# One layer stack on one core: S5's direct term inside its kernels, z in three matmuls, S5's steps a head later, the border's chunks behind the scale

## The chip, the core and the metric

The kernel runs on one core of a Trainium2 chip. The metric is the device time of one execution in microseconds; the time of a kernel is the median over its runs. The engines named below are PE (TensorE, the matmuls), DVE (VectorE), ACT (ScalarE), POOL (GpSimd) and SP (SyncE, which issues most of the loads). Each works through its own queue in order, and waits on semaphores for the others.

## The reference

A batch of one, 256 positions of 2048 features, goes through four layers with a different mixer each. After each mixer stands a residual sum and a layer norm:

```python
for i in range(DEPTH):
    out = (ssd_mixer, fox_mixer, mla_mixer, s5_mixer)[i](h, ...)
    h = layer_norm(ALPHA * h + out, ln_g[i], ln_b[i])
```

SSD is a state-space mixer with a causal convolution and a chunked scan, Fox is attention with a cumulative forget gate, MLA is attention with low-rank queries and keys. The change touches S5 most:

```python
u, z = jnp.split(h @ w_in, 2, axis=-1)
lam_bar = jnp.exp(lam * step)
bu = jnp.einsum('gpi,btgi->btgp', b_bar, u.reshape(bsz, T, GROUPS, GROUP))
states = scan of  s[t] = lam_bar * s[t-1] + bu[t]          # complex, 64 states in each of 128 groups
y = einsum('gip,btgp->btgi', c, states).real.reshape(bsz, T, WIDTH) + d_skip * u
y = gelu(y)
y = y * sigmoid(y @ w_glu + b_glu)
y = y * silu(z)
return y @ w_out
```

The term `d_skip * u` is called the direct term below.

## The kernel before

**Matmuls.** Every product is made in three parts: a weight is split into a high and a low half (`whi` on ACT, L119; `wlo` on DVE, L120), the activations are split as well (`h`, two tiles that lie side by side), and high times high, high times low and low times high are summed. `half` loads one half of a weight tile (512 KB) into one of seven `raw` buffers and splits it; there are four `whi` and four `wlo`. `proj_T` makes an output with features on the partitions: per block of 128 inputs a matmul of 512 columns (L147: the high weight against both halves of the activations) and one of 256 (L148), into a PSUM tile `pT` whose two halves DVE then adds (L157). `proj_tok` makes outputs with positions on the partitions, in three matmuls of 512 columns (L126 to L128), in four column blocks `cb`. `proj_Tk` uses three matmuls of 256 columns (L212 to L214, tiles `pk`).

**The order of the work.** The program is written out once, in one order. Each `tick` (one half tile of weights) runs what had been deferred to it: `C.defer(n, fn)` runs `fn` n ticks later, and `C.behind` issues it behind the last matmul. Each engine then gets its own queue from that, so what is issued earlier stands ahead on its engine.

**Borders.** `out_layer` ends each layer: the output projection, the residual sum `resid` (L309) with statistics (L310), the scale `nm` from a Newton iteration on DVE (`stats`, rows `nt`, `ny`), `norm` in two passes over chunks of blocks (first pass L339 with the mean, second pass L340 with the scale `ny`), and the transposition for the next layer (`ptr`, L353, on PE; high half on ACT; low half `h` on DVE, L357). In the next layer's first projection PE has its first matmuls of L126 and L127 among the ptr, but L128 needs the low halves. Position block t = 1 comes last.

**SSD.** Per group of heads, `scores` multiplies the decays with the products of c and b (`cbp`, L567), `turn_x` transposes x (`xp`).

**S5's kernels, made during Fox.** `s5_params` is a generator that POOL, DVE and PE work through while Fox's heads run: in each of 16 groups POOL makes powers (`pn`, L1130 to L1139), and `turn` has PE transpose them and multiply them out (`wp`, L1070; `kp`, L1077) into the kernels of the short-range convolution (`kt`, stored to DRAM as K_d). The steps are called by `next(steps)`: one behind each of the last v strips (stripes of Fox's value projection), then one per head.

**S5's own stage.** Four strips `ft` of u are projected and turned; the scan over the states runs on DVE (tiles `X`, `sc`, L1207 to L1213), in pieces, `advance` issuing `SCAN_US` of it per tick; meanwhile PE makes the 16 tiles of z. Per strip, outputs of two kinds are summed: `near` from the short kernels (matrices `shifts`, from K_d) and `far` from the states (matrices `mats`, from P_d; the addition into `ys` is L1416). Then `back1` transposes (`yp`, L1425), ACT copies to `yt`, `back2` transposes again (`yp`, L1435), DVE adds the direct term (L1441), ACT takes gelu (L1450) and the result is split (L291, L292). The z tile is summed by L157, goes through tanh on ACT and a product on DVE (L1337). After the 16 tiles come the 16 of the gate (glu), then the output projection.

Of the kernel before, what the change touches and what calls it, by code (L numbers as in the profile page):

```python
# [30 lines left out]
class Core:  # L31
# [127 lines left out]
    def proj_tok(self, srcs, aT, n=512, before=None, tail=None, spare=None):  # L159
# [10 lines left out]
        while h < N:  # L170
# [123 lines left out]
    def out_layer(self, li, parts, gb_tiles, spare, out=None):  # L294
# [12 lines left out]
        def resid(t, cb, ps):  # L307
            r = self.hres[:, t, cb * 512:(cb + 1) * 512]
            V.scalar_tensor_tensor(r, r, ALPHA, ps, op0=ALU.mult, op1=ALU.add)  # L309
            V.bn_stats(st[:, t, cb, :], r)  # L310

        def stats(t):
            mv = self.tp.tile([P, 2], F32, tag="mv", name="mv", bufs=2)
            V.bn_aggr(mv, st[:, t])
# [6 lines left out]
            V.scalar_tensor_tensor(nm[t], mv[:, 0:1], -1.0, rs[t], op0=ALU.mult, op1=ALU.mult)  # L321
# [72 lines left out]
        for k0, nk in ((0, 2), (2, 2), (4, 4), (8, 4), (12, 4)):  # L394
            norm(1, k0, nk, 3)
# [55 lines left out]
def ssd(C, hT, out):  # L451
# [3 lines left out]
    with C.tc.tile_pool(name="ssd", bufs=1) as sp, C.tc.tile_pool(name="ssd_c", bufs=1) as vp, C.tc.tile_pool(name="ssd_t", bufs=1) as tp:  # L455
# [87 lines left out]
        def group(g):  # L543
# [111 lines left out]
def fox(C, hT, out):  # L655
# [3 lines left out]
    with pool(name="fox", bufs=1) as fp, pool(name="fox_t", bufs=2) as tp, \  # L659
# [49 lines left out]
        def head(h):  # L709
# [237 lines left out]
def s5_params(C, sp, sq):  # L947
# [118 lines left out]
    def turn(n, st, pn, d):  # L1066
# [5 lines left out]
        nc.scalar.copy(wt, wp.rearrange("p q b c f -> p (q b c f)"))  # L1072
        kp = C.aux("kp")
        for qq in range(2):
            for e in range(2):
                for c in range(2):
                    nc.tensor.matmul(kp[32 * qq:32 * qq + 32, e * 64:(e + 1) * 64], d[:, 2 * qq + e, c],  # L1077
                                     pn[:, c, 2 * qq + e, 0:4].rearrange("p r i -> p (r i)"), start=c == 0, stop=c == 1)
# [75 lines left out]
def s5(C, hT, out):  # L1154
# [8 lines left out]
    with C.tc.tile_pool(name="s5", bufs=1) as sp, C.tc.tile_pool(name="s5_w", bufs=1) as wp, C.tc.tile_pool(name="s5_t", bufs=1) as tp:  # L1163
        dT = sp.tile([P, KB], F32, name="dT")
        bg = sp.tile([P, KB], F32, name="bg")
        nc.sync.dma_start(dT, A["s5_dT"])
# [415 lines left out]
```

## Time and profile before

| | us |
|---|---|
| median of 3 runs | 2019.85 (2015.91 to 2023.44) |
| the profiled execution's own time | 2021.63 |
| its span, first to last instruction | 2019.8 |
| PE busy | 1970.5 (98%) |
| DVE busy | 1470.2 (73%) |
| ACT busy | 956.4 (47%) |
| POOL busy | 410.1 (20%) |
| mean granted TensorE clock | 0.991 |

The stages stand one after the other: SSD to about 709 us, Fox to 1233, MLA to 1581, S5 to the end; within S5 the u strips run from about 1600 to 1696, the z tiles to about 1826. Matmuls overlap, so the busy time of one is longer than the distance to the next; from which of the two a cost is worked out is said each time. A window's row has the busy time and the number of instructions of each engine, then the granted clock (1.00 is full speed), the DMA share and the rate. A row of the waits has the total, the number of times and the longest.

### The profile page before, as it was taken

What the parts mean: (1) busy time and instruction counts of PE and PEld (TensorE: products, weight loads), DVE (VectorE), ACT (ScalarE), POOL (GpSimd) and SP (SyncE); (2) the same over time, 40 slices, a digit from 0 to 9 for tenths busy, and PEclk for the clock granted to TensorE, in tenths of its full rate; (3) what the DMA queues carried; (4) which work ended last, traced back from release to release, by engine and by line L of the source; (5) the groups of instructions that cost most, each with busy time, mean ns of one, the idle gap of its engine ahead of it and who ended that gap; (6) DMA issues with size and microseconds to landing.
All of it is one profiled execution on the core that took longest, in us unless ns stands there. A gap on an engine that the chain in (4) does not pass through costs nothing.

```text
span 2019.8 us, 32021 instructions
## 1 busy us (share of the span) xinstructions
PE 1970.5 (98%) x12169; PEld 1684.2 (83%) x12169; DVE 1470.2 (73%) x2572; ACT 956.4 (47%) x1427; POOL 410.1 (20%) x482
## 2 busy tenths in 40 slices
PE   8999999999999999999999999999999999999997
PEld 6788888888888878788888888988988799878885
DVE  6788788887654596577777567666666778997856
ACT  5455555655433434344444443544654355445442
POOL 0101111011100027999993000000000000110002
PEclk9999999999999999999999999999999999999999
DMA  8555555555665546566566564655357456586552
GB/s 286 185 178 182 183 181 190 178 185 181 206 218 188 185 151 230 179 204 200 199 198 212 173 204 127 207 186 176 126 172 245 175 182 196 169 249 215 193 192 91
DMA packets 116235, 382.42 MB, mean 189 GB/s; under 512 B 18208, under 2 KB 20976, under 8 KB 114288
## 3 DMA queue, kind: packets, MB, share of 16 engines
q1 hardware_dynamic: 103424, 348.11, 52.0%
q0 software_dynamic: 7808, 26.56, 4.2%
q10 hardware_dynamic: 4848, 5.70, 0.8%
q8 instruction: 96, 1.57, 0.3%
q14 instruction: 59, 0.48, 0.1%
HBM read 366.20 MB, written 14.11 MB: 188 GB/s over the span
## 4 chain that ended last, share of the span: by engine, by line
PE 82%; DVE 10%; DMA 3%; POOL 2%; issue 2%; ACT 1%; SPq 0%; DVEq 0%; POOLq 0%; ACTq 0%
PE pT L147 24%; PE pT L148 12%; PE pt L127 10%; PE pt L128 10%; PE pt L126 10%; DVE wlo L120 3%; PE pk L212 2%; PE pk L214 2%; PE pk L213 2%; PE yd L602 1%; DVE hres L339 1%; DVE hres L340 1%; PE o L444 1%; DMA raw<-in_ssd_z 1%; PE kp L1077 1%
## 5 line engine op out<-in xcount | busy, mean ns | idle before, releaser
L120 DVE TENSOR_TENSOR wlo<-raw,whi 128x1024 fp32r<-128x1024 f32 (+4 forms) x612 | 749.5, 1227 | 350.1 <-ACT whi L119 343.7
L119 ACT CAST whi<-raw 128x1024 fp32r<-128x1024 f32 (+4 forms) x612 | 631.3, 1036 | 731.9 <-PE pt L128 320.7
L147 PE MATMUL pT<-h,whi 128*128 128x512 f32 (+2 forms) x2080 | 746.5, 401 | 0.0
L148 PE MATMUL pT<-h,wlo 128*128 128x256 f32 (+2 forms) x2080 | 585.7, 282 | 1.5 <-DVE wlo L120 1.5
L147 PEld LDWEIGHTS pT<-h,whi 128*128 128x128 f32 (+2 forms) x2080 | 389.9, 187 | 94.4 <-issue 0.2
L148 PEld LDWEIGHTS pT<-h,wlo 128*128 128x128 f32 (+2 forms) x2080 | 392.2, 189 | 3.2 <-DVE wlo L120 2.3
L126 PE MATMUL pt<-whi,h 128*128 128x512 f32 (+2 forms) x716 | 281.1, 393 | 6.3 <-ACT whi L119 6.0
L127 PE MATMUL pt<-wlo,h 128*128 128x512 f32 (+2 forms) x716 | 280.0, 391 | 5.8 <-DVE wlo L120 5.6
L128 PE MATMUL pt<-whi,h 128*128 128x512 f32 (+2 forms) x716 | 277.6, 388 | 0.3 <-DVE h L357 0.3
L127 PEld LDWEIGHTS pt<-wlo,h 128*128 128x128 f32 x716 | 136.4, 190 | 35.5 <-DVE wlo L120 8.9
L126 PEld LDWEIGHTS pt<-whi,h 128*128 128x128 f32 x716 | 136.2, 190 | 34.5 <-ACT whi L119 6.4
L128 PEld LDWEIGHTS pt<-whi,h 128*128 128x128 f32 x716 | 136.3, 190 | 26.7 <-issue 1.7
L589 POOL TENSOR_TENSOR xs<-xs,dsk 128x512 f32<-128x512 f32 x16 | 20.8, 1316 | 373.5 <-ACT xs L585 373.5
L126 PE MATMUL pt<-whi,yh 128*128 128x512 f32 x240 | 95.5, 398 | 0.0
L127 PE MATMUL pt<-wlo,yh 128*128 128x512 f32 x240 | 95.4, 397 | 0.0
L128 PE MATMUL pt<-whi,yl 128*128 128x512 f32 x240 | 94.9, 395 | 0.0
L147 PE MATMUL pT<-y,whi 128*128 128x512 f32 x256 | 90.9, 400 | 0.0
L1179 POOL DMA_DIRECT2D mats<-W_d x8 | 4.3, 542 | 336.1 <-DVE h L292 265.7
L148 PE MATMUL pT<-y,wlo 128*128 128x256 f32 x256 | 72.0, 281 | 0.0
L496 DVE SCALAR_TENSOR_TENSOR conv<-u,cw,conv 128x255 f32<-128x255 f32 x144 | 68.8, 479 | 2.2
L89 POOL MEMSET mask<- 128x256 f32 x2 | 0.6, 314 | 302.1 <-PE pt L128 164.4
L147 PEld LDWEIGHTS pT<-y,whi 128*128 128x128 f32 x256 | 48.1, 188 | 12.0 <-DVE y L292 0.2
(469 smaller groups left out, 3050.3 us busy)
## 6 DMA issues: line engine op xcount, KB each, us to landing
raw<-in_ssd_x SPq DMA_DIRECT2D x64, 512.0 KB
raw<-in_ssd_o SPq DMA_DIRECT2D x64, 512.0 KB
raw<-in_ssd_z SPq DMA_DIRECT2D x63, 512.0 KB
raw<-in_fox_v SPq DMA_DIRECT2D x32, 512.0 KB
raw<-in_fox_q SPq DMA_DIRECT2D x32, 512.0 KB
raw<-in_fox_k SPq DMA_DIRECT2D x32, 512.0 KB
raw<-in_fox_z SPq DMA_DIRECT2D x32, 512.0 KB
raw<-in_fox_o SPq DMA_DIRECT2D x32, 512.0 KB
```

The costliest lines, as they stand in the source:

```text
L119: nc.scalar.copy(hi[:, c], r[:, c])
L120: nc.vector.tensor_tensor(lo[:, c], r[:, c], hi[:, c], op=ALU.subtract)
L126: mm(ps, s[0], m[0], start=first, stop=False)
L127: mm(ps, s[0], m[1], start=False, stop=False)
L128: self.last = mm(ps, s[1], m[0], start=False, stop=last).ins
L147: mm(ps, hi, hT[2][order[kb]], start=kb == 0, stop=False)
L148: self.last = mm(ps[:, 0], lo, hT[0][order[kb]], start=False, stop=kb == KB - 1).ins
L212: mm(o, ws[0], a[0], start=kb == 0 and c % 2 == 0, stop=False)
L213: mm(o, ws[0], a[1], start=False, stop=False)
L214: self.last = mm(o, ws[1], a[0], start=False, stop=end).ins
L496: nc.vector.scalar_tensor_tensor(c[:, k:], u[:, 0:T - k], cw[:, ti, 3 - k:4 - k], c[:, k:], op0=ALU.mult, op1=ALU.add)
L589: nc.gpsimd.tensor_tensor(heads(xs[c]), heads(xs[c]), bc(dsk, g), op=ALU.mult)
```

## The change

1. **Direct term in the kernels.** The first 16 rows of `kt` get `eye * skip` added, where `skip` is a new table of d_skip (input `s5_dk`), so that `near` already contains `d_skip * u`. L1441 and its table `dT` go; gelu reads `yp3` from PSUM directly, one tick earlier (the step `gelu` is merged into `back2`). `kp` is laid out over 128 partitions, with a tile position for each matmul, and `kt` is filled by a copy and a multiply-add.
2. **z in three matmuls.** New `proj_T3`: three matmuls of 256 columns per block, summed in PSUM (`zps`); L157 falls away there, and tanh and the product read PSUM.
3. **S5's steps a head later:** no `next(steps)` in head 0.
4. **Borders:** only the first chunk of position block 1 is normed ahead; the others are issued behind the scale (`issue_after(self.scaled)`). The last run of weights of the last column block is multiplied in two column parts of 256, and `resid` and its statistics for t = 1 follow in halves.
5. **S5's outputs:** `SCAN_US` 2.2 for 1.9; the matrices of the last strip get a tile of their own (`mats3`) and are waited for differently (`wait`); `finish` comes one tick after, not three.
6. **SSD:** the scores of group 0 are deferred by 6 ticks, not 3.

```diff
+    def proj_T3(self, src, hT, ps):
+        for i in range(2):
+            w = self.half(src, i)
+            for j in range(8):
+                kb = 8 * i + j
+                self.mm3(ps, [x[:, j * P:(j + 1) * P] for x in w], [x[kb] for x in hT[0:2]], kb == 0, kb == KB - 1)
+            self.tick()
...
+                parts = [slice(0, n)]
+                if last and r == len(runs) - 1:
+                    parts = [slice(0, n // 2), slice(n // 2, n)]
...
+            self.scaled = V.scalar_tensor_tensor(nm[t], mv[:, 0:1], -1.0, rs[t], op0=ALU.mult, op1=ALU.mult).ins
...
-        for k0, nk in ((0, 2), (2, 2), (4, 4), (8, 4), (12, 4)):
-            norm(1, k0, nk, 3)
+        norm(1, 0, 2, 3)
+        with self.tc.issue_after(self.scaled):
+            for k0, nk in ((2, 2), (4, 4), (8, 4), (12, 4)):
+                norm(1, k0, nk, 3)
...
-            C.defer(3, scores)
+            C.defer(3 if g else 6, scores)
...
-            C.behind(lambda: next(steps, None))
+            if h:
+                C.behind(lambda: next(steps, None))
...
-        V.tensor_copy(kt[n % 2][:, :, 48:], kp[0:64, 0:128].rearrange("p (e f) -> p e f", e=2))
+        V.tensor_copy(kt[n % 2][:, 64:], kp[:, 16:64])
+        V.scalar_tensor_tensor(kt[n % 2][:, 48:64], eye, skip[:, n:n + 1], kp[:, 0:16], op0=M, op1=Ad)
...
         def z_tile(kb):
-            C.proj_T(A["s5_z"][kb], hT, zs[kb])
+            zps = C.acc("zps")[:, 0:T]
+            C.proj_T3(A["s5_z"][kb], hT, zps)
             th = tp.tile([P, T], F32, tag="th", name="th", bufs=3)
-            nc.scalar.activation(th, zs[kb], AF.Tanh, scale=0.5)
-            nc.vector.scalar_tensor_tensor(zs[kb], th, 1.0, zs[kb], op0=ALU.add, op1=ALU.mult)
+            nc.scalar.activation(th, zps, AF.Tanh, scale=0.5)
+            nc.vector.scalar_tensor_tensor(zs[kb], th, 1.0, zps, op0=ALU.add, op1=ALU.mult)
...
-            wait = 4 if k == 6 else 3 if k < 6 else 1
+            wait = 4 if k == 6 else 5 if k == 7 else 3
...
-                    dst = yf[gq].rearrange("p (r c) -> p r c", r=L)
-                    nc.vector.scalar_tensor_tensor(dst, uX[ft][:, :, gq], dT[:, kb:kb + 1], src[:, a], op0=ALU.mult, op1=ALU.add)
-            C.defer(1, lambda: gelu(ft, yf))
+                    nc.scalar.activation(g.rearrange("p (m k r) -> p r k m", k=4, r=L), src[:, a], AF.Gelu_apprx_tanh)
+                    C.split(yh[kb], yl[kb], g)
...
-SCAN_US = 1.9
+SCAN_US = 2.2
```

In the order of the instructions the change shows itself as follows. On PE, at the end of Fox's v strips, before: the last matmuls of the strip, the second group of transposes and products of S5's powers, and the third group right behind it.

```order
L126 MATMUL pt_7235<-whi,h_6497 128x512
L127 MATMUL pt_7235<-wlo,h_6497 128x512
L128 MATMUL pt_7235<-whi,h_6497 128x512
L1070 MATMUL wp<-ident,wn 128x2x64 x4
L1077 MATMUL kp<-pn,bd_6979 32x64 x8
L1070 MATMUL wp<-ident,wn 128x2x64 x4
L1077 MATMUL kp<-pn,bd_6978 32x64 x8
L147 MATMUL pT<-h_6344,whi 128x512
L148 MATMUL pT<-h_6344,wlo 128x256
```

And now, at the same place, head 0's first projection follows the second group at once:

```order
L127 MATMUL pt_7257<-wlo,h_6508 128x512
L128 MATMUL pt_7257<-whi,h_6508 128x512
L1093 MATMUL wp<-ident,wn 128x2x64 x4
L1102 MATMUL kp<-pn,bd_6990 32x64 x8
L147 MATMUL pT<-h_6347,whi 128x512
L148 MATMUL pT<-h_6347,wlo 128x256
L147 MATMUL pT<-h_6347,whi 128x512
```

The third group stands after head 0's three projections (96 rows) and its logits (`lps`), ahead of head 1's first projection:

```order
L148 MATMUL pT<-h_6508,wlo 128x256
L743 MATMUL lps<-fox_k,fox_q 128x128
L744 MATMUL lps<-fox_k,fox_q 128x128
L745 MATMUL lps<-fox_k,fox_q 128x128
L1093 MATMUL wp<-ident,wn 128x2x64 x4
L1102 MATMUL kp<-pn,bd_6989 32x64 x8
L147 MATMUL pT<-h_6347,whi 128x512
L148 MATMUL pT<-h_6347,wlo 128x256
```

The third wp/kp group has moved one head further on.

On DVE, at the first border, position block 1, before: the first passes (L339, the wide ones) stand in the gaps of the Newton iteration, and the second passes follow the scale.

```order
L339 SCALAR_TENSOR_TENSOR hres<-hres,mean,gb_5920 128x512
L243 TENSOR_SCALAR nt<-ny,ve 128x1
L339 SCALAR_TENSOR_TENSOR hres<-hres,mean,gb_5960 128x512
L244 TENSOR_SCALAR ny<-nt,ny 128x1
L339 SCALAR_TENSOR_TENSOR hres<-hres,mean,gb_6000 128x512
L243 TENSOR_SCALAR nt<-ny,ve 128x1
L1011 MEMSET pw 128x64
L244 TENSOR_SCALAR ny<-nt,ny 128x1
L321 SCALAR_TENSOR_TENSOR nm<-mv,ny 128x1
L340 SCALAR_TENSOR_TENSOR hres<-hres,ny,gb_5900 128x256 x2
```

And now (first passes L353, second passes L354, low halves L371):

```order
L335 SCALAR_TENSOR_TENSOR nm<-mv,ny 128x1
L354 SCALAR_TENSOR_TENSOR hres<-hres,ny,gb_5902 128x256
L353 SCALAR_TENSOR_TENSOR hres<-hres,mean,gb_5882 128x256
L353 SCALAR_TENSOR_TENSOR hres<-hres,mean,gb_5922 128x512
L354 SCALAR_TENSOR_TENSOR hres<-hres,ny,gb_5902 128x256
L354 SCALAR_TENSOR_TENSOR hres<-hres,ny,gb_5942 128x512
L353 SCALAR_TENSOR_TENSOR hres<-hres,mean,gb_5962 128x512
L353 SCALAR_TENSOR_TENSOR hres<-hres,mean,gb_6002 128x512
L354 SCALAR_TENSOR_TENSOR hres<-hres,ny,gb_5982 128x512
L354 SCALAR_TENSOR_TENSOR hres<-hres,ny,gb_6022 128x512
L371 TENSOR_TENSOR h_6347<-ptr,h_6347 128x2x128 x2
```

Four of the five first passes have moved from ahead of the scale to behind it; the low halves still follow all second passes.

On DVE, in the z tiles, ahead of the second pair of additions into ys, before:

```order
L120 TENSOR_TENSOR wlo<-raw,whi 128x1024
L1207 TENSOR_TENSOR sc<-X_16055,a4s 128x512
L1209 TENSOR_TENSOR sc<-X_16055,a4s 128x512
L157 TENSOR_REDUCE zs_15320<-pT 128x256
L1211 TENSOR_TENSOR sc<-sc 128x512
L1337 SCALAR_TENSOR_TENSOR zs_15320<-th,zs_15320 128x256
L1213 TENSOR_TENSOR X_16055<-X_16055,sc 128x64x8
L120 TENSOR_TENSOR wlo<-raw,whi 128x1024
L1416 TENSOR_TENSOR ys<-ys,far_17236 128x4x64
L1416 TENSOR_TENSOR ys<-ys,far_17237 128x4x64
```

And now (the scan is L1232 to L1238, the product L1363, the additions L1444):

```order
L120 TENSOR_TENSOR wlo<-raw,whi 128x1024
L1232 TENSOR_TENSOR sc<-X_16127,a4s 128x512
L1234 TENSOR_TENSOR sc<-X_16127,a4s 128x512
L1236 TENSOR_TENSOR sc<-sc 128x512
L120 TENSOR_TENSOR wlo<-raw,whi 128x1024
L1238 TENSOR_TENSOR X_16127<-X_16127,sc 128x64x8
L1363 SCALAR_TENSOR_TENSOR zs_15377<-th,zps 128x256
L1444 TENSOR_TENSOR ys<-ys,far_17378 128x4x64
L1444 TENSOR_TENSOR ys<-ys,far_17379 128x4x64
```

The reduction has gone; up to this place both kernels have issued 14 wlo since the scan of this piece began, and the new one four scan rows of 512 more.

More of the change, by code (lines that the diff above doesn't have):

```diff
@@ L1061, in s5_params @@
     bd = [sq.tile([P, 4, 2, 32], F32, name=f"bd{n}") for n in range(2)]
-    kt = [sq.tile([64, 2, 112], F32, name=f"kt{n}") for n in range(2)]
+    kt = [sq.tile([P, 112], F32, name=f"kt{n}") for n in range(2)]
+    eye, skip = sq.tile([P, 16], F32, name="eye"), sq.tile([P, 16], F32, name="skip")
+    nc.sync.dma_start(skip, A["s5_dk"])
+    V.tensor_tensor(eye, C.ident[:, 0:16], C.ident[:, 16:32], op=Ad)
+    for k0 in range(32, P, 16):
+        V.tensor_tensor(eye, eye, C.ident[:, k0:k0 + 16], op=Ad)
     for t in bd + kt:
@@ L1346, in y_load @@
             tm = shifts(ft, h2)
-            pm = mats(C.P_d[ft].rearrange("p h c j f -> p h (c j f)")[:, 2 * h2:2 * h2 + 2]).rearrange(
-                "p (g c q e f) -> p g c q e f", g=2, c=2, q=2, e=2)
-            held.append((k, C.now, tm, pm))
+            src = C.P_d[ft].rearrange("p h c j f -> p h (c j f)")[:, 2 * h2:2 * h2 + 2]
+            if ft < 3:
+                pm = mats(src)
+            else:
+                if h2 == 0:
+                    rest.append(sp.tile([P, 2, 1024], F32, tag="XA", name="mats3"))
+                pm = rest[0][:, h2]
+                nc.gpsimd.dma_start(pm, src)
+            held.append((k, C.now, tm, pm.rearrange("p (g c q e f) -> p g c q e f", g=2, c=2, q=2, e=2)))
         def outputs():
             k, since, tm, pm = held[0]
-            wait = 4 if k == 6 else 3 if k < 6 else 1
+            wait = 4 if k == 6 else 5 if k == 7 else 3
             if C.now >= since + wait and (k > 5 or PIECE[k // 2] in done):
@@ L1369, in outputs @@
                     rest.append(pm)
-                    if held:
-                        held[0] = (7, C.now) + held[0][2:]
-                    else:
-                        C.defer(3, finish)
+                    if not held:
+                        C.defer(1, finish)
             if held:
                 C.defer(1, outputs)
-        rest = []
         def finish():
@@ L1430, in back2 @@
         def back2(ft, yt):
-            yf = [yt[:, gq // 2].rearrange("p r g i -> p (r g i)")[:, gq % 2 * T:(gq % 2 + 1) * T] for gq in range(4)]
+            y4 = sp.tile([P, 2, 4, T], F32R, tag=f"xu{ft}", name=f"y4{ft}")
             for hq in range(2):
```

52 lines of the change are left out of this document (23 added, 29 removed).

## The prediction

> **What bounds the kernel now.** I read the page's first part, then the list of PE's waits, then the windows around the long waits, and last the queue of the engine that was waited for.
>
> ```profile
> PE 1970.5 (98%) x12169; PEld 1684.2 (83%) x12169; DVE 1470.2 (73%) x2572; ACT 956.4 (47%) x1427; POOL 410.1 (20%) x482
> ...
> PE pt L127 <- DVE wlo L120: 6.5, 5, 3.3
> ...
> PE ptr L353 <- DVE hres L340: 5.5, 2, 2.8
> PE far L1412 <- DVE yt L1441: 3.0, 1, 3.0
> PE kp L1077 <- POOL pn L1132: 2.8, 1, 2.8
> PE yp L1425 <- DVE ys L1416: 2.8, 1, 2.8
> PE far L1412 <- DMA mats<-P_d: 2.3, 1, 2.3
> PE kp L1077 <- POOL pn L1139: 2.2, 1, 2.2
> PE pt L128 <- DVE h L357: 1.8, 2, 1.6
> PE pT L148 <- DVE wlo L120: 1.5, 1, 1.5
> ```
>
> PE is the bound nearly everywhere, so the change can win only what PE waits (us in total, times, longest), and what the clock loses behind such a wait. The waits that the change touches are two at the first Fox head (kp, 5.0 us), four in the z tiles (3.0, 2.8, 2.3 and 1.5, together 9.6 us), those of the borders (5.5 and 1.8 us) and the longest one on wlo, in the first SSD group (3.3 us).
>
> **S5's steps a head later.** The end of the v strips, in windows, with the rows of POOL and of PE:
>
> ```profile
> 816.94:820.35 3.41, 0.30 (x2) 0.14 (x2) 0.63 (x1) 0.26 (x1) 3.25 (x4) 1.00 0.68 225
> 820.35:823.77 3.42, 2.94 (x19) 2.58 (x20) 0.28 (x1) 0.00 (x0) 3.33 (x7) 0.50 0.49 129
> 823.77:827.18 3.41, 3.41 (x12) 2.83 (x12) 0.00 (x0) 0.00 (x0) 3.02 (x8) 0.50 0.29 95
> 827.18:830.59 3.41, 3.41 (x21) 2.99 (x20) 1.53 (x2) 1.48 (x2) 3.27 (x5) 1.00 0.03 8
> ...
> 816.57 1.72 POOL L1132 TENSOR_TENSOR pn<-t,t 128x320 f32<-128x320 f32 x1
> 819.92 0.86 POOL L1139 TENSOR_TENSOR pn<-t,t 128x320 f32<-128x320 f32 x1
> 822.23 0.74 POOL L714 TENSOR_TENSOR ckm<-ck,mask 128x256 f32<-128x256 f32 x1
> ...
> 818.34 0.30 PE L1077 MATMUL kp<-pn,bd 128*32 128x64 f32 x2 [2.79 <-POOL pn L1132]
> 820.83 0.96 PE L1077 MATMUL kp<-pn,bd 128*32 128x64 f32 x11 [2.19 <-POOL pn L1139]
> ```
>
> The third wp/kp group stands in PE's queue right behind the second, while POOL, busy 3.25 of 3.41 us, is still making its powers. PE waits 2.79 + 2.19 = 5.0 us. The columns after the window are busy us of PE, PEld, DVE, ACT and POOL, then the granted clock: 0.50 in the two windows behind the wait, where PE was busy 2.94 + 3.41 = 6.35 us and so lost half, 3.2 us. With the group moved behind head 1's start, PE works on head 0's q first and comes to kp one head later; the order shows head 0's three projections (96 rows, some 17 us by the 0.357 us per pair that is measured below) and its logits ahead of it. POOL's powers are done by 820.8 on its own pace. So both go: -8.2 us, at least -5.0 if the clock drops anyway, at most -8.2. What else moves: ckm of head 1 now stands ahead of POOL's next group, 0.74 us, which has a head of slack; the table loads on SP move with it; kt's copy is now a copy and a multiply-add, some 0.2 us more DVE in each of 16 groups, while DVE is busy 1.5 of 3.41 us. I cost these at nothing; that slack is their cover, and without it the 0.74 us would show once.
>
> The Trainium skill (TensorE: Matmul & The Clock Gate, "Why this matters for your kernels") says that the clock halves after an idle window of 3.4 us and asks for no gaps above 3 us. The window length agrees with the 3.41 us here; the threshold does not, since 0.30 us of work in the window was not enough to keep the clock. By the page alone the clock loss would have another cause and stay.
>
> **The z tiles.** DVE and PE from the start of the z tiles, in one window and by line:
>
> ```profile
> 1690.00:1820.00 130.00, 122.73 (x1367) 107.74 (x1367) 127.10 (x278) 62.78 (x101) 13.26 (x22) 0.99 0.71 207
> ...
> L120 DVE TENSOR_TENSOR wlo<-raw,whi 128x1024 fp32r<-128x1024 f32 x34 | 41.4, 1217 | 0.4 <-ACT whi L119 0.4
> L157 DVE TENSOR_REDUCE zs<-pT 128x256 f32<-128x512 f32 x16 | 10.9, 682 | 0.0
> ...
> L1207 DVE TENSOR_TENSOR sc<-X,a4s 128x512 f32<-128x512 f32 x13 | 8.9, 684 | 0.1
> ...
> L1337 DVE SCALAR_TENSOR_TENSOR zs<-th,zs 128x256 f32<-128x256 f32 x16 | 6.7, 417 | 0.0
> ...
> L1441 DVE SCALAR_TENSOR_TENSOR yt<-xu,dT,yp 128x256 f32<-128x256 f32 x12 | 5.0, 474 | 0.0
> ...
> 1741.95:1745.36 3.41, 3.30 (x13) 3.04 (x14) 3.34 (x5) 1.17 (x2) 0.00 (x0) 0.50 0.66 244
> ...
> 1742.06 1.51 PE L1425 MATMUL yp<-ident,ys 128*128 128x128 f32 x6 [2.76 <-DVE ys L1416]
> ...
> 1750.78 1.28 ACT L1450 ACT_TABLE_LOAD   x1 [2.48 <-DVE yt L1441]
> ```
>
> DVE is busy 127 of 130 us here: it is the bound of this stretch, and PE's 9.6 us of waits, with 1.65 us lost to the clock at 1741.95 (half of 3.30), 11.3 us in all, are the most that the edits can win. DVE's rows overlap by about 0.08 us, so a 682 ns row costs its queue 0.60. The change takes away 16 reductions (16 x 0.60 = 9.6 us) and 16 direct terms (16 x 0.39 = 6.3 us; the row counts the 12 in its window), and the z product now reads PSUM, nearest to L1441's 474 against 417 ns: 16 x 0.06 = +1. So DVE sheds 14.9 us. That is more than PE waits, but the scan's share per step rises from 1.9 to 2.2 us, and it matters what stands ahead of each row that PE waits for.
>
> I counted DVE's rows in the order, up to the second pair of far additions, on which the first yp waits. Both kernels have 14 wlo there; five reductions go (-3.0 us), five products grow (+0.3) and four more scan rows of 512 come ahead (4 x 0.60 = +2.4). That is 0.3 us earlier, and PE comes 0.3 us later: the wait of 2.8 us shrinks to about 2.2. Up to the fourth pair, ten reductions and four direct terms go (-7.6), two wlo fewer (-2.3) and 15 scan rows of 32 more (some 0.18 each, +2.7) stand ahead: 7 us earlier. But PE comes to that yp three half tiles (8.6 us) earlier than before, since the faster scan lets the outputs start sooner. A yp that waits for nothing now will wait about 2. The third I put at 1, and 0.5 for the PSUM buffers that gelu now holds. The P_d wait of 2.3 us goes, as these matrices get a tile of their own and load before. Together 5.7 us of waits stay of 9.6: -3.9. Whether the clock drops behind the shorter first wait is open: half of 1.65, -0.8.
>
> Three matmuls of 256 columns replace 512 + 256. An unbroken run of each kind, first and last row:
>
> ```profile
> 1660.09 0.28 PE L214 MATMUL pk<-h,wlo 128*128 128x256 f32 x1
> ...
> 1671.97 0.28 PE L214 MATMUL pk<-h,wlo 128*128 128x256 f32 x1
> ...
> 1833.55 0.40 PE L147 MATMUL pT<-y,whi 128*128 128x512 f32 x1
> ...
> 1844.98 0.40 PE L147 MATMUL pT<-y,whi 128*128 128x512 f32 x1
> ```
>
> 33 triples in 11.88 us are 0.360 us each, 32 pairs in 11.43 us are 0.357: 256 x 0.003 = +0.8 us. This is the busy time's trap: mean durations of 280 to 400 ns overlap, and by them three would cost 0.16 us more per block, 42 us in all, which starts exclude. The Trainium skill (same page, "Back-to-back issue gap") gives N/2.4 + 2.5 ns per matmul, an estimate of 2.5 ns per block from one more issue, +0.6 us; the rows here say the same within their rounding. The z stage gives -3.9 - 0.8 + 0.8 = -3.9 us; bounds -10.5 (all waits and the clock go) and +2 (none go, and the clock drops once more at 1.65).
>
> **Borders and last runs.** Border 1, DVE and PE:
>
> ```profile
> 719.19 0.16 DVE L321 SCALAR_TENSOR_TENSOR nm<-mv,ny 128x1 f32<-128x1 f32 x1
> 719.27 2.86 DVE L340 SCALAR_TENSOR_TENSOR hres<-hres,ny,gb 128x256 f32<-128x256 f32 x5
> ...
> 719.89 0.81 PE L353 MATMUL ptr<-ident,hres 128*128 128x128 f32 x4 [2.80 <-DVE hres L340]
> ...
> 722.85 0.77 PE L128 MATMUL pt<-whi,h 128*128 128x512 f32 x1
> ...
> 2006.71 0.69 DVE L309 SCALAR_TENSOR_TENSOR hres<-hres,pt 128x512 f32<-128x512 f32 x1 [3.41 <-PE pt L128]
> 2007.43 0.69 DVE L310 BATCH_NORM_STATS2 bnst<-hres 128x6 f32<-128x512 f32 x1
> ```
>
> The scale nm is now ready some 1.7 us sooner, as the wide first passes no longer fill its chain, and the first ptr comes at about 718.2. But L128 needs h, whose additions stand behind all second passes on DVE. The five second passes take 2.86 us, one of 256 columns about 0.4; the first passes of the later chunks, as many and as wide, some 2.4 us, now stand behind the scale instead of in its gaps. What the scale gains (1.7) they take back, with the split rows of the last run, so that DVE finishes about 0.4 us later: +0.4. I walked border 2 the same way to +0.6 and border 3 to -0.6. The halves of the last run cost 6 more matmuls in each of four layers and split rows on DVE, +0.1 each. In the last layer, where nothing else is left to do, the sum and the statistics of 0.69 us each (the two rows at the end) wait for the last matmul with 256 columns instead of 512, about 0.47 by L1441's row: -0.4. Sum of the borders +0.4 (0.4 + 0.6 - 0.6), of the last runs 0.0: +0.4, between -3 (PE's 5.5 us halved) and +3.5 (one more half-clock window and a longer chain).
>
> **SSD scores six steps later.** The wait of 3.3 us on wlo has two products ahead of it on DVE:
>
> ```profile
> 72.54 2.35 DVE L567 TENSOR_TENSOR arena<-arena,cbp 128x1024 f32<-128x1024 f32 x2
> ```
>
> The order shows both products still ahead of that wlo, and the 16 rows of L538 ahead of them, as now; the matmul of cbp goes later on PE, and xp comes before the wait: +0.3, between -2.3 (both products gone from ahead) and +2 (they come later than the wlo would).
>
> **The sum.** -8.2 - 3.9 + 0.4 + 0.3 = -11.4 us on the profiled execution's 2021.6 us; that lies 1.8 us above the runs' median, 2019.85, so 2008.5.
>
> **The rivals.**
> - *All waits in the z tiles go.* DVE's 14.9 us exceed the 11.3 that PE loses, which speaks for it; the places counted above speak against. Then -8.2 - 10.5 and the borders' -3: about 1998. Chance 0.15.
> - *The z tiles' waits only move.* The scan is ahead of wlo by 0.3 us more per half tile of 2.86 us (8 x 0.357), and yp comes earlier. S5 gives 0 to +2: 2012.5 to 2014.5. Chance 0.22.
> - *The clock falls at Fox for another reason.* If a window with 0.30 us of work in it kept the clock, the two windows at 0.50 would have another cause and stay; that both follow such a window here and at the first yp speaks against it. -5.0 instead of -8.2: 2011.7. Chance 0.07. The Trainium skill's threshold, above, reads so.
> - *Slower: each strip's yp waits as the first does.* DVE is full, and the outputs come three half tiles earlier. Four times (2.76 + 1.65) = 17.6 us, and gelu holding PSUM through a table load adds 1.3 at each (the table load of 1.28 us at 1750.78), 22.8 against 11.3: +11.5, + 0.8, + 0.7 at the borders and SSD, -8.2 at Fox: +4.8, 2024.7. It decides from about 4.5 us per strip on. Against it: DVE is 7 us further on by the second yp. Chance 0.06.
>
> My forecast has 0.50, own range 2004 to 2012. A measurement of this kernel tells about 0.5% (10 us) from no change: below 2009.75 is faster. Four fifths of my case and the first rival lie there: 0.55. Slower has 0.06, the rest, 0.39, is within. The range 1999 to 2016 leaves out the slower case and the ends of two rivals.
>
> **What would show it.** Right: no wait of kp at the first head, and clock 1.00 between 815 and 830; no wait on P_d; waits of yp on ys that are about 2 us, at the first and the second strip; ptr earlier, but L128 as late as now. Wrong: any wait of kp on pn at head 1 (then Fox's 8.2 us fail); yp waits above 4 us or new 0.50 windows in the z tiles; zps starts above 0.120 us apart; L128 at the borders a us earlier or later.

## The result, and the profile after

The changed kernel takes 1998.96 us (median of 4 runs, 1996.52 to 2000.24) against 2019.18 for the kernel before on the same chip (2015.91 to 2023.44): a ratio of 0.9905, 95% interval 0.9886 to 0.9924, some 20 us. Timed once more, it was 1996.64 against 2020.11, 0.9888 (0.9867 to 0.9909). The forecast was 2008.5, a gain of 11.4 us: the sign is right and the gain is nearly twice as large. The time lies at the very lower edge of the range (1999 to 2016) and 5 us below the forecast's own range (2004 to 2012). The profiled execution took 1999.25 us, its span is 1997.5. One execution of the experiments below, of e7, took 2177.8 us at a mean granted clock of 0.832; it stands in no range and no ratio below.

The page's first line and the list of PE's waits of the changed kernel (us in total, times, longest):

```profile
PE 1957.1 (98%) x12449; PEld 1690.2 (85%) x12449; DVE 1468.9 (74%) x2583; ACT 954.4 (48%) x1427; POOL 410.8 (21%) x482
...
PE pt L126 <- ACT whi L119: 5.6, 2, 5.3
PE ptr L367 <- DVE hres L354: 5.6, 7, 1.4
PE xp L592 <- DVE xc L515: 3.3, 2, 2.8
PE pt L127 <- DVE wlo L120: 3.0, 6, 0.7
PE yp L1453 <- DVE ys L1444: 2.9, 2, 2.3
PE ptr L367 <- DVE h L371: 2.8, 1, 2.8
PE yp L1453 <- DVE sc L1236: 2.0, 1, 2.0
```

The waits of kp, of far on P_d and on `yt`, and pT's on wlo are gone. The wait of 3.3 us on wlo in SSD went too, but xp now waits 2.8 there. New is one of 2.8 us on `h` at a border. The whole list sums to 35.8 us before and 26.9 after: 8.9 us of waits do not explain 20.

To see where the rest went, each execution is cut at the first ptr of each of the three borders, which stands ahead of everything that the border's change moves, and at the start of the last matmul (us; here and in the table of the experiments, differences of times rounded to a tenth):

| profiled execution | start to border 1 | to border 2 (v strips, Fox) | to border 3 (MLA) | to the last matmul (S5) |
|---|---|---|---|---|
| before | 709.2 | 521.6 | 350.9 | 424.6 |
| after | 704.8 | 502.7 | 355.2 | 421.3 |
| difference | -4.4 | -18.9 | +4.3 | -3.3 |

Fox wins 18.9 where 8.2 was forecast, SSD 4.4 where 0.3 was to be lost, and MLA loses 4.3. One trace of each kernel is not enough to trust every tenth here: the SSD stage, which the same kernel runs in 709.2 and 706.1 us in two traces of the kernel before, moves by some 3 us between executions.

**Fox.** At the place of the old kp waits, the windows of the changed kernel (busy us of PE, PEld, DVE, ACT, POOL, then the granted clock, DMA share, rate):

```profile
813.40:816.80 3.40, 3.40 (x21) 2.97 (x20) 1.86 (x3) 1.45 (x2) 3.24 (x4) 1.00 0.54 177
816.80:820.20 3.40, 3.40 (x22) 2.96 (x21) 1.64 (x2) 1.68 (x2) 3.32 (x5) 1.00 0.60 194
820.20:823.60 3.40, 3.40 (x21) 2.96 (x21) 2.65 (x3) 1.08 (x2) 3.38 (x5) 1.00 0.88 278
```

PE is full and the clock stays at 1.00, while POOL works through its powers as before. Then come two things that nobody waits for. One of the 16 groups of kp, before and after, each with the row that follows (start, us, engine):

```profile
842.60 0.89 PE L1077 MATMUL kp<-pn,bd 128*32 128x64 f32 x16
843.41 0.50 PE L147 MATMUL pT<-h,whi 128*128 128x512 f32 x1
```

```profile
828.62 0.43 PE L1102 MATMUL kp<-pn,bd 128*32 128x64 f32 x16
828.98 0.49 PE L147 MATMUL pT<-h,whi 128*128 128x512 f32 x1
```

The same 16 matmuls hold PE 0.81 us before and 0.36 after; in 16 groups that is some 7 us. And an unbroken tile of a Fox projection, its second and its last matmul of 512 columns, before and after:

```profile
893.44 0.39 PE L147 MATMUL pT<-h,whi 128*128 128x512 f32 x1
...
898.38 0.40 PE L147 MATMUL pT<-h,whi 128*128 128x512 f32 x1
```

```profile
896.80 0.40 PE L147 MATMUL pT<-h,whi 128*128 128x512 f32 x1
...
901.65 0.40 PE L147 MATMUL pT<-h,whi 128*128 128x512 f32 x1
```

Fourteen pairs take 4.94 us before and 4.85 after: 353 and about 347 ns per pair. The edit leaves this code alone, and the durations in the rows are nearly the same; the distance of the starts shows it. SSD's output projection does so as well, at 233 and 229 ns per matmul (rows below, with the experiment that turns it).

**z tiles.** PE's far and yp before, then after, by line (busy, mean ns, then idle time before and what ended it):

```profile
L1412 PE MATMUL far<-X,mats 64*64 64x64 f32 x512 | 10.0, 220 | 5.3 <-DVE yt L1441 3.0 <-DMA mats<-P_d 2.3
L1425 PE MATMUL yp<-ident,ys 128*128 128x128 f32 x32 | 5.2, 303 | 2.8 <-DVE ys L1416 2.8
```

```profile
L1440 PE MATMUL far<-X,mats 64*64 64x64 f32 x512 | 9.7, 220 | 0.1
L1453 PE MATMUL yp<-ident,ys 128*128 128x128 f32 x32 | 4.7, 275 | 4.9 <-DVE ys L1444 2.9 <-DVE sc L1236 2.0
```

far hardly waits any more (0.1), yp waits 2.1 us longer in all, 2.3 at the first strip and 2.0 at the second. The clock is lost once here, as before, now behind the second yp:

```profile
1756.03:1759.44 3.41, 3.41 (x19) 3.41 (x18) 3.10 (x14) 0.51 (x2) 0.00 (x0) 0.50 0.37 147
```

**Border 2.** The changed kernel's first and last ptr with the wait on `h` between them, and the windows around it:

```profile
1207.51 0.63 PE L367 MATMUL ptr<-ident,hres 128*128 128x128 f32 x4
...
1221.50 1.11 PE L367 MATMUL ptr<-ident,hres 128*128 128x128 f32 x4 [2.76 <-DVE h L371]
1229.11 0.60 PE L367 MATMUL ptr<-ident,hres 128*128 128x128 f32 x4
...
1216.72:1220.13 3.41, 1.57 (x11) 0.94 (x9) 3.41 (x7) 1.33 (x3) 1.28 (x2) 1.00 0.07 6
1220.13:1223.54 3.41, 2.04 (x8) 2.04 (x9) 3.41 (x13) 0.59 (x1) 0.00 (x0) 0.50 0.00 0
1223.54:1226.96 3.42, 3.42 (x12) 3.42 (x12) 2.05 (x5) 1.60 (x2) 0.00 (x0) 0.50 0.18 24
```

The wait lasts from 1218.74 to 1221.50. PE has 1.57 us of work in the window in which it begins, and the clock is halved for the two windows that follow. Half of what PE is busy there, (2.04 + 3.42) / 2 = 2.7 us, is lost to the clock: this border is the one place where the change costs several microseconds.

### The profile page after: what moved, and what is told of

Same layout as the page of the kernel before. It is cut to its first block, busy times and chain, and to the rows that moved or that the text cites. A ratio compares the mean times of both kernels' runs of the same rounds, so it can differ in the third digit from the quotient of the medians.

```text
span 1997.5 us, 32606 instructions
## 1 busy us (share of the span) xinstructions
PE 1957.1 (98%) x12449; PEld 1690.2 (85%) x12449; DVE 1468.9 (74%) x2583; ACT 954.4 (48%) x1427; POOL 410.8 (21%) x482
## 4 chain that ended last, share of the span: by engine, by line
PE 83%; DVE 12%; DMA 2%; issue 2%; ACT 1%; SPq 0%; DVEq 0%; ACTq 0%; POOLq 0%
PE pT L147 22%; PE pT L148 11%; PE pt L128 11%; PE pt L127 11%; PE pt L126 11%; DVE wlo L120 3%; PE pk L223 2%; PE pk L224 2%; PE pk L225 2%; PE yd L618 1%; DVE hres L354 1%; DVE hres L353 1%; DMA raw<-in_ssd_z 1%; PE o L460 1%; PE zps L126 1%
## 5 line engine op out<-in xcount | busy, mean ns | idle before, releaser
L147 PE MATMUL pT<-h,whi 128*128 128x512 f32 (+1 forms) x1824 | 645.9, 398 | 0.0
L148 PE MATMUL pT<-h,wlo 128*128 128x256 f32 (+1 forms) x1824 | 509.3, 279 | 0.0
L147 PEld LDWEIGHTS pT<-h,whi 128*128 128x128 f32 (+1 forms) x1824 | 340.0, 186 | 79.6
L148 PEld LDWEIGHTS pT<-h,wlo 128*128 128x128 f32 (+1 forms) x1824 | 341.3, 187 | 1.0
L128 PE MATMUL pt<-whi,h 128*128 128x512 f32 (+2 forms) x716 | 278.0, 388 | 0.3 <-DVE h L371 0.3
L128 PEld LDWEIGHTS pt<-whi,h 128*128 128x128 f32 x716 | 136.9, 191 | 27.3 <-issue 1.9
L128 PE MATMUL pt<-whi,yl 128*128 128x512 f32 x240 | 94.5, 394 | 0.0
L126 PE MATMUL zps<-h,whi 128*128 128x256 f32 x256 | 74.9, 293 | 0.0
L128 PE MATMUL zps<-h,wlo 128*128 128x256 f32 x256 | 73.1, 286 | 0.0
L127 PE MATMUL zps<-h,whi 128*128 128x256 f32 x256 | 73.1, 285 | 0.0
```

The lines of the kernel that those rows point to most:

```text
L126: mm(ps, s[0], m[0], start=first, stop=False)
L127: mm(ps, s[0], m[1], start=False, stop=False)
L128: self.last = mm(ps, s[1], m[0], start=False, stop=last).ins
L147: mm(ps, hi, hT[2][order[kb]], start=kb == 0, stop=False)
L148: self.last = mm(ps[:, 0], lo, hT[0][order[kb]], start=False, stop=kb == KB - 1).ins
```

## The experiments

Expectations speak of "the kernel before" and "the changed kernel"; edits are against the one that is named. Times are medians, ratios are to the runs of the kernel before on the same chip, with their 95% intervals. The profiled executions cut as above:

| | border 1 | border 2 | border 3 | last matmul |
|---|---|---|---|---|
| before again (e1) | 706.1 | 520.6 | 349.5 | 426.7 |
| before, a head later (e3) | 703.7 | 511.7 | 350.6 | 423.7 |
| before, kp's layout (e4) | 708.0 | 514.5 | 350.5 | 423.1 |
| before, statistics tile (e5) | 704.5 | 518.7 | 351.7 | 426.9 |
| before, two parts (e6) | 706.8 | 521.0 | 349.2 | 427.1 |
| before, e3 + e4 + e5 (e10) | 701.5 | 502.0 | 353.7 | 424.4 |
| after again (e2) | 705.0 | 503.8 | 355.6 | 424.5 |
| after, old borders (e7) | 703.4 | 502.3 | 352.1 | 421.1 |
| after, old z (e8) | 703.1 | 502.8 | 355.2 | 419.2 |
| after, padded (e9) | 705.6 | 503.4 | 354.2 | 423.0 |
| after, old borders and z (e11) | 705.5 | 502.9 | 353.5 | 421.1 |
| after again (e12) | 702.3 | 504.9 | 355.4 | 424.6 |

**The two kernels again.** Neither is edited.

> The kernel before, unchanged, to see what of the difference between the two traces repeats. Theory 'program': the pace of unbroken matmul stretches belongs to the program, so Fox's pT tiles take 5.73 to 5.75 us each again (353 ns per pair), SSD's output matmuls 233 ns. Theory 'run': the pace is drawn per execution, and some stages show 347 ns and 229 ns as the changed kernel's trace did. Either way the waits repeat: kp 2.8 + 2.2 us, yp 2.8, far 3.0 and 2.3.

2018.21 us. Fox's projections ran at 353 to 354 ns in all but two tiles and SSD's output at 233, as in the first trace; MLA's projections ran at 347 in 12 tiles of 13, where the first trace had 353. So part of the paces belongs to the program, and MLA's pT to the execution.

> The changed kernel, unchanged. Theory 'program': Fox's pT tiles 5.63 us (347 ns per pair) again. Theory 'run': the pace differs from the first trace in at least one stage. About 1999 us by either.

2004.21 us; 347 in Fox and 229 in SSD's output again. The 5 us over the first profile stand in the S5 part (424.5 against 421.3) and in Fox (503.8 against 502.7), and the mean granted clock is 0.989 against 0.993.

**One part alone: S5's steps a head later.** Kernel before with

```diff
-            C.behind(lambda: next(steps, None))
+            if h:
+                C.behind(lambda: next(steps, None))
```

> The kernel before with one edit: no S5 step in head 0. My prediction's step: -8.2 us (5.0 of waits and 3.2 of clock), so about 2011, kp waits gone, clock 1.00 at 815 to 830. Rival: the waits go but the time stays within 3 us of before because other waits take their place at head 1. Rival 'pace': more than -12 us, with pT pairs at 347 ns in Fox.

2008.74 us, ratio 0.9952 (0.9936 to 0.9969): about -10. The same place in its trace, in one window, has PE full at full clock:

```profile
815.40:818.80 3.40, 3.40 (x21) 2.93 (x20) 1.70 (x2) 1.10 (x2) 3.38 (x6) 1.00 0.84 243
```

From border 1 to border 2 it takes 8.9 us less than e1. Fox's pace stays at 353 to 354 ns. In the five traces with the third group in head 0 (before, e1, e4, e5, e6) the clock is at 0.50 for two windows, 6.83 us, at this place; in the nine without it, it is 1.00 from 790 to 860 us. This step of the prediction (-8.2) is shown.

**One part alone: kp's layout.** Kernel before with the new layout of `kp`, its tile positions, the loop order that goes with them, and one copy into `kt`; no direct term.

```diff
-        for qq in range(2):
+        for c in range(2):
             for e in range(2):
-                for c in range(2):
-                    nc.tensor.matmul(kp[32 * qq:32 * qq + 32, e * 64:(e + 1) * 64], d[...], ..., start=c == 0, stop=c == 1)
+                for qq in range(2):
+                    r0 = 64 * e + 32 * qq
+                    nc.tensor.matmul(kp[r0:r0 + 32, 0:64], d[...], ..., start=c == 0, stop=c == 1, tile_position=(0, r0))
```

> The kernel before with one edit: kp laid out over 128 partitions with tile positions, c outermost, one copy into kt; no direct term. I costed this at nothing. Theory from the two traces: each group's 16 rows take 0.36 instead of 0.82 us, 16 x 0.46 = -7.4 us at most, -6.5 if the two groups that wait for POOL gain nothing: about 2012. Rival: the group's time is hidden and the kernel is unchanged within 2 us. Rival 'pace': -12 us or more with pT pairs at 347 ns.

2011.74 us, ratio 0.9967 (0.9954 to 0.998): about -7. Three groups of its trace, with kp's waits in brackets:

```profile
812.87 0.43 PE L1078 MATMUL kp<-pn,bd 128*32 128x64 f32 x16
816.71 0.32 PE L1078 MATMUL kp<-pn,bd 128*32 128x64 f32 x8 [1.95 <-POOL pn L1134]
819.20 0.44 PE L1078 MATMUL kp<-pn,bd 128*32 128x64 f32 x8 [2.17 <-POOL pn L1141]
840.30 0.43 PE L1078 MATMUL kp<-pn,bd 128*32 128x64 f32 x16
```

The waits of the third group are still there; every group is as short as in the changed kernel. From the first to the last start of a group are 0.67 us before and 0.21 here, 16 x 0.46 = 7.4 us in all: the gain needs no wait. Whether the tile position alone or the order of the loop with it does it was not tried apart.

**One part alone: the statistics tile.** It has two buffers of 192 B per partition in the kernel before and one of 288 B after, so everything allocated behind it lies 96 B lower. Kernel before with

```diff
-        st = self.tp.tile([P, 2, 4, 6], F32, tag="bnst", name="bnst")
+        st = self.tp.tile([P, 12, 6], F32, tag="bnst", name="bnst", bufs=1)
```

> The kernel before with one edit that moves no instruction: the statistics tile is one buffer of 288 bytes per partition in place of two of 192, so that every tile allocated behind it lies 96 bytes lower. Theory 'address': the matmul pace hangs on where tiles lie, and SSD's output matmuls (yh lies behind it) go from 233 to 229 ns and Fox's pT pairs from 353 to 347 ns, about -9 us. Rival 'instruction stream': no address matters, both paces stay (233, 353) and the time is unchanged within 2 us.

2016.33 us, ratio 0.9991 (0.9978 to 1.0004): nothing that can be told in the time, and not the 9 us of the theory. But SSD's output ran at 229 ns in 25 stretches of 26, Fox's projections at 347 in 16 tiles and at 353 to 354 in 15. No instruction differs there. MLA's `pk` went the other way: 384 of them take 46.93 us from start to start, 44.89 in e1. So the place of the tiles gives some 3 us in SSD's output (some 760 steps, 4.3 ns each) and takes 2.0 in MLA.

**One part alone: the last run in two parts.** Kernel before with the `parts` of the diff above, without the split of `resid`.

> The kernel before with one edit: the last run of each layer in two column parts, 12 matmuls of 256 in place of 6 of 512; sums and statistics as before. Theory 'instruction stream': 6 more matmuls per layer shift everything behind on PE, and Fox's pT pairs go from 353 to 347 ns, about -6 us; SSD's output, ahead of it, stays at 233. Rival 'address': both stay and the time rises by 0 to 1 us (0.1 us per layer).

2019.24 us, ratio 1.0002 (0.9989 to 1.0016), paces as in the kernel before: this part costs nothing that the time resolves (some 3 us), and a changed stream of instructions is not enough to turn the pace.

**Undoing the border's order.** Changed kernel with

```diff
-        norm(1, 0, 2, 3)
-        with self.tc.issue_after(self.scaled):
-            for k0, nk in ((2, 2), (4, 4), (8, 4), (12, 4)):
-                norm(1, k0, nk, 3)
+        for k0, nk in ((0, 2), (2, 2), (4, 4), (8, 4), (12, 4)):
+            norm(1, k0, nk, 3)
```

> The changed kernel with the border's chunks in the old order (all first passes in the gaps of the Newton iteration), all else as changed. My prediction's step: the new order is worth +0.4 us, so this would be 0.4 us faster, with PE's waits at each border in one piece of about 3 us again. Rival 'the order helps': 2 to 5 us slower. Rival from the two traces (border 2 took 3.3 us longer): 2 to 4 us faster, most of it at border 2.

Runs of 1994.19 to 1997.15 us, ratio 0.9889 (0.9861 to 0.9917); the interval includes the changed kernel's 0.9905 and 0.9888, so the time decides between none of the three. Border 2 in its trace, first and last ptr and the windows of PE between them, the first being the one with the least work:

```profile
1205.74 0.63 PE L367 MATMUL ptr<-ident,hres 128*128 128x128 f32 x4
...
1224.11 0.60 PE L367 MATMUL ptr<-ident,hres 128*128 128x128 f32 x4
...
1211.74:1215.15 3.41, 1.77 (x13) 1.44 (x12) 3.41 (x10) 0.59 (x1) 0.00 (x0) 1.00 0.00 0
1215.15:1218.57 3.42, 3.19 (x21) 2.87 (x22) 3.38 (x8) 0.65 (x2) 1.28 (x2) 1.00 0.05 5
```

The waiting is in pieces of at most 1.6 us and the clock stays. At borders 1 and 3 the old order has its wait in one piece of 2.8 us, as expected, where the new one has pieces of at most 1.4; at border 2 it is the other way round. From the one ptr to the other border 2 takes 18.37 us; in the changed kernel, by the rows shown with the result, 21.60, in the kernel before (1230.79 to 1249.04) 18.25. In all five traces with the new order (after, e2, e8, e9, e12) the granted clock is 0.50 behind this wait, for 6.83 us in four of them and 3.41 in e8; half of PE's busy time there is 2.7 to 2.9 us in the four and 1.7 in e8. In the nine with the old order it is 1.00 over the whole border.

**Undoing z in three matmuls.** Changed kernel with

```diff
-            zps = C.acc("zps")[:, 0:T]
-            C.proj_T3(A["s5_z"][kb], hT, zps)
+            C.proj_T(A["s5_z"][kb], hT, zs[kb])
```

and tanh and the product on `zs[kb]`, as before.

> The changed kernel with z by 512 + 256 columns and DVE's sum of the halves, as before; direct term, gelu from PSUM and the faster scan stay. My prediction's step: three matmuls cost PE 0.8 us and save DVE 16 x 0.60 = 9.6 us, so this one waits some 3 to 6 us longer in the z tiles and is 2 to 5 us slower. Rival: DVE had enough slack from the direct term alone, the same time within 1 us. Rival 'clock': new half-speed windows in the z tiles and 8 us or more.

1997.47 us, ratio 0.9896 (0.9877 to 0.9916), between the two timings of the changed kernel. Its waits in the z tiles:

```profile
PE yp L1452 <- DVE ys L1443: 4.6, 2, 3.3
...
PE far L1439 <- issue: 0.3, 1, 0.3
```

With 9.6 us of reductions back on DVE, yp waits 4.6 us where 4.9 were, and far 0.3; the clock is at 0.50 for 6.83 us around the first yp (from 1719.77), in the traces of the changed kernel for 3.41 or 6.83 us in the z tiles. The S5 part, 419.2 us, is the shortest of all. The waits that were expected to grow by 3 to 6 us did not, and the expectation of 2 to 5 us slower is missed, though the interval of the time alone would leave some room for it. What is left of the change in S5 (direct term, gelu from PSUM, scan, `mats3` and `wait`) is enough for what the waits won; which of these does it was not tried apart.

**The place undone.** Changed kernel, its statistics tile padded to 384 B:

```diff
-        st = self.tp.tile([P, 12, 6], F32, tag="bnst", name="bnst", bufs=1)
+        st = self.tp.tile([P, 16, 6], F32, tag="bnst", name="bnst", bufs=1)
```

> The changed kernel with its statistics tile padded from 288 to 384 B per partition (nothing reads the padding), so that every tile allocated behind it lies 96 B higher, as in the kernel before. Theory (the pace of an unbroken stretch of matmuls hangs on where the tiles lie): SSD's output projection goes back from 229 to 233 ns per matmul of 512 columns (+2.9 us there), Fox's projections from 347 to 353 ns per pair in half or all of the tiles (+3 to +6.6 us); in all 2002 to 2008 us, against 1999.0 for the changed kernel as it is. Rival (the pace comes from the changed stream of instructions, or is drawn anew in every program): 229 and 347 ns stay, 1998 to 2000.

2000.9 us, ratio 0.9899 (0.988 to 0.9917): below the theory's 2002 to 2008, and not to be told from the changed kernel by the time. The paces can be told. SSD's output, the first and last rows of a stretch: the kernel before (73 steps), the changed kernel (75), the padded one (74).

```profile
594.81 0.40 PE L128 MATMUL pt<-whi,yl 128*128 128x512 f32 x1
...
611.84 0.40 PE L126 MATMUL pt<-whi,yh 128*128 128x512 f32 x1
```

```profile
594.68 0.39 PE L126 MATMUL pt<-whi,yh 128*128 128x512 f32 x1
...
611.84 0.39 PE L126 MATMUL pt<-whi,yh 128*128 128x512 f32 x1
```

```profile
594.72 0.40 PE L128 MATMUL pt<-whi,yl 128*128 128x512 f32 x1
...
611.99 0.40 PE L127 MATMUL pt<-wlo,yh 128*128 128x512 f32 x1
```

17.03 / 73 = 233, 17.16 / 75 = 229, 17.27 / 74 = 233 ns. `pk` is back at 44.87 us for the 384, Fox at 353 to 354 in 15 tiles of 33 (347 in 18). Over all 14 traces, SSD's output has 229 and `pk` 46.9 wherever the tiles lie 96 B lower, and 233 and 44.9 to 45.0 wherever they do not. So these two paces hang on the place. For Fox the place is only part of it: 353 to 354 in all tiles of before, e1, e3, e4 and e6 but two, about half of them in e5 and e9, one at most where the lower place and kp's layout (whose `kt` is 448 B smaller in each of two buffers) come together. Which operand's place matters was not found; no run moves one operand alone.

**Three edits alone.** Kernel before with e3, e4 and e5 together.

> The kernel before with three edits and nothing else: no S5 step in head 0, kp over 128 partitions with a tile position each, and the statistics tile in one buffer of 288 B. Theory (these three carry the whole gain, and add up): 2018.5 - 9.7 - 6.7 - 1.6 = 2000.5, down to 1995.5 if all of Fox's projections run at 347 ns a pair. Rival (the two edits of the S5 steps win the same waits twice): the layout is worth 16 x 0.46 = 7.4 us without any wait, and the kp waits are gone anyway, so 2003 to 2006 would be left. Second rival (the z tiles, borders and outputs carry part of the gain): above 2004, with the four waits of the z tiles as before.

2000.05 us (1996.97 to 2004.14), ratio 0.99 (0.9881 to 0.992). The theory named 2000.5. From border 1 to 2 its trace has 502.0 us; e1's 520.6 with what e3, e4 and e5 win alone there (8.9, 6.1 and 1.9) would be 503.7, and Fox runs at 347 ns in all tiles but one. The waits of the z tiles are those of the kernel before:

```profile
PE far L1415 <- DVE yt L1444: 3.1, 1, 3.1
...
PE yp L1428 <- DVE ys L1419: 2.6, 1, 2.6
PE far L1415 <- DMA mats<-P_d: 2.4, 1, 2.4
```

Two small edits of S5's kernel making and 96 B of place carry as much as the whole change, as far as the width of the runs lets one say.

**Both undone.** Changed kernel with e7's and e8's edits.

> The changed kernel with two of its parts undone: the border's chunks all normed ahead as before, and z by 512 and 256 columns with DVE's reduction. Theory (both parts cost or are worth nothing): 1999.0 - 2.8 (borders) - 1.5 (z) = 1994.7; it beats both kernels. Rival (three matmuls pay once the borders are as before, or the borders' gain was a chance of the clock): 1997 to 2000.

1997.52 us, ratio 0.9885 (0.9868 to 0.9901). Not the 1994.7 of the theory; it beats the kernel before, but not the changed one, timed beside it:

> The changed kernel unchanged, timed once more beside the others on the same chip. Theory: 1999 (1996.5 to 2001), ratio 0.990 to the kernel before, 3 to 5 us above the version with two parts undone. Rival (a chip's own half-speed stretches decide): 2001 to 2004, as its second execution (2004.2) had it.

1996.64 us (1995.24 to 2002.48), ratio 0.9888 (0.9867 to 0.9909). The two cannot be told apart. The 3 us that border 2 costs in the traces are no more than the width of the runs, and what else undoing both costs stays open; one piece is a wait of 3.0 us at far that came back in e11.

## Why the prediction was right in sign and short by half

- **S5's steps a head later, -8.2: right.** e3 measured about -10 in the time and -8.9 in the stage; the full upper bound was won, since the clock stayed at 1.00. The rival that the clock falls there anyway is refuted. The Trainium skill (TensorE: Matmul & The Clock Gate, "Why this matters for your kernels") asks for no gaps above some 3 us, and by its letter two waits of 2.79 and 2.19 us would not have been the cause of the clock's fall, which would have stayed. The trace sided with the row: 0.30 us of work in a window of 3.41 did not keep the clock.
- **"The change can win only what PE waits": the step that failed.** The layout of `kp` stands in the change and in no term of the sum; it measured -7 (e4), while kp's waits at the first head were still there (1.95 and 2.17 us). The view that would have shown it was at hand: 16 matmuls in 0.81 us, 0.05 us each, all work of PE on its path. I looked at kp only as something that waits. The Trainium skill (TensorEngine Tiling (Array Packing), "Theoretical Speedup") gives up to four times for a dimension of at most 32, which the 32 columns of the stationary operand are; here the distance of the starts fell by 0.67 / 0.21 = 3.2. That sentence belonged in the prediction as a rival.
- **Paces of unbroken stretches: no term of the sum.** The prediction took 0.357 us per pair as given. SSD's output won some 3 us and `pk` lost 2.0, both shown as an effect of place; Fox's pT won the 2 to 4 us that e5 and e10 show beyond the other terms (33 tiles of 16 pairs, 6 ns each, are 3.2 us). The profile before shows both 347 and 353 ns within one program, but nothing in it says which edit would turn them.
- **z tiles, -3.9: about right, for half the reason.** Over the seven traces with the new S5 stage (two of them with the old z) the stretch from border 3 to the end is 422.1 us in the mean, over the seven with the old one 425.2: -3.1, with border 3 and the gate's tiles in it. The waits went as forecast: 4.9 us at yp, about 2 at the first and second strip, none on P_d (in e2, e9 and e12 it is 1 at the second and 2 at the third). The clock was not won: one window at 0.50 in the z tiles of the profile after as in the one before, one or two in the other traces of the new stage, one to four in those of the old. And the step that counted the reductions as DVE's gain and let it shrink the waits failed: e8 puts them back and the waits stay. The triples do start 0.360 us apart, as forecast, but the unbroken pairs of z in e8 are 347 to 354 ns, not 357, so that three matmuls cost PE some 2.5 us by these rows (256 x 0.010), not 0.8.
- **Borders, +0.4: right at border 1, mis-sized at border 2.** PE at border 1 of the changed kernel:

```profile
704.78 1.34 PE L367 MATMUL ptr<-ident,hres 128*128 128x128 f32 x8
...
713.68 0.41 PE L367 MATMUL ptr<-ident,hres 128*128 128x128 f32 x2 [0.98 <-DVE hres L354]
...
718.69 0.79 PE L128 MATMUL pt<-whi,h 128*128 128x512 f32 x1 [0.28 <-DVE h L371]
```

  At border 1 the first ptr of block 1 comes 1.8 us earlier against the border's start (10.71 to 8.90 us), and the L128 that waits for the low halves stands 13.67 us after that start before (709.18 to 722.85) and 13.91 now: +0.24 for +0.4. At border 2 +0.6 was forecast and +3.3 measured (18.25 to 21.60): the wait, which had been in pieces, became one of 2.76 us and took the clock with it, 2.7 us. Without that, the +0.6 of the walk along DVE is what is left. The bound "one more half-clock window" had the mechanism and one window where there were two. The time of the whole kernel does not resolve it.
- **Last runs, 0:** nothing to be seen in e6, which leaves out the split of `resid`. The -0.4 in the last layer does not show: from the start of the last matmul to the end it is 13.56 us before and 13.50 after. **SSD scores, +0.3:** the wait of 3.3 us on wlo went and one of 2.8 at xp stands there, a wash as forecast. The clock behind that wait was in no term; it is at 0.50 for 6.83 us in the first trace of before (from 76.25) and for 3.41 in that of after (from 76.67), but not at all in e1 and e8, so the edit cannot be credited with it. The stage's gain that repeats is the pace.
- **Where luck comes in.** The time is the 1998 of the first rival (all waits in the z tiles go, chance 0.15), but these waits did not go; kp's layout and the paces, which nobody forecast, filled the place.

So of about 20 us won, kp's waits and clock are 9, kp's layout 7, the z stage about 3, the paces of SSD's output and Fox 5 to 7; border 2 and `pk` take back 3 and 2. The first two are shown by runs of their own (e3, e4); the others are read from the traces, since the times of e5, e7 and e8 do not resolve them.

## What to carry to other kernels

Before an edit is costed at nothing, multiply its instructions by the distance of their starts in the trace: a bystander of 0.8 us that stands 16 times on the bound engine's path is worth more than a wait of 5 us. Compare paces of unbroken stretches, not only waits, between two traces, and when they differ where the code does not, suspect where the tiles lie. When a wait is moved, ask whether it grows together with others: a single wait of nearly 3 us with little work around it cost the clock as well, the same waiting spread over more windows did not.

## What the runs showed of the hardware

**Pace by place.** Matmuls with nothing to wait for run at a few fixed paces: 229 or 233 ns per 512 columns in SSD's output, 347, 350 or 353 ns per pair elsewhere. 96 B of allocation turned the first both ways. MLA's pT changed between executions of one program (353 and 347), so place is not all of it.

**The same wait with and without the clock's fall.** The first yp of a strip in the changed kernel, in two executions (the first profile, then e12), each with two windows of 3.41 us around the wait:

```profile
1722.93 0.85 PE L1453 MATMUL yp<-ident,ys 128*128 128x128 f32 x6 [2.30 <-DVE ys L1444]
...
1718.49:1721.90 3.41, 2.14 (x19) 1.90 (x17) 3.38 (x6) 1.05 (x2) 0.00 (x0) 1.00 0.97 256
1721.90:1725.31 3.41, 2.38 (x21) 2.41 (x22) 3.34 (x7) 1.37 (x3) 0.00 (x0) 1.00 1.00 284
```

```profile
1724.35 0.85 PE L1453 MATMUL yp<-ident,ys 128*128 128x128 f32 x6 [2.32 <-DVE ys L1444]
...
1721.68:1725.09 3.41, 1.09 (x11) 0.88 (x10) 3.41 (x7) 1.34 (x2) 0.00 (x0) 1.00 1.00 252
1725.09:1728.50 3.41, 3.41 (x18) 3.41 (x18) 3.31 (x6) 1.07 (x3) 0.00 (x0) 0.50 0.95 357
```

The windows are not chosen freely. In each of the 14 traces all falls of the clock begin a whole number of 3.413 us apart; in the first profile of the changed kernel they begin at 76.67, 718.37, 1220.13, 1575.12, 1756.03 and 1988.13, which are 188, 335, 439, 492 and 560 such steps from the first. On this grid the wait of the first execution is cut in two: PE keeps 2.14 us of work in one window and 2.38 in the next, and the clock stays. In the second execution the whole wait, 1722.03 to 1724.35, lies in one window, 1.09 us of work are left in it, and the next window runs at 0.50. The Trainium skill (TensorE: Matmul & The Clock Gate, "What's actually happening") says that the window of activity runs freely and does not start anew with a kernel; the grid agrees with that, and makes such a wait cost its clock in some executions and not in others.

It is also a good part of the width of the runs. Of the nine executions of the changed kernel the slowest (2004.21 us) has a mean granted clock of 0.989, the next two (2002.48 and 2000.24) 0.991; 0.995 and 0.996 stand at 1997.68, 1995.24 and 1995.60. In the 38 executions of the kernel before that were timed beside the experiments, the 16 with 0.991 or less take 2020.5 us in the mean, the 11 with 0.993 or more 2015.1.
